# Seven products for the attention projection, its sums made behind the convolution's, and an accumulating transfer in place of the add

## Chip, cores, metric

One core of one Trainium2 chip. The metric is the device time of one execution in microseconds (us).

## What is computed

One decoder layer on 512 rows of 2048 channels, in float32. The parts that the change touches are these lines of the reference:

```python
z = jnp.einsum('bsd,dc->bsc', h, w_in[l])
cb, cc, cv, q, k, v, f_logit, gate_c, gate_a = jnp.split(z, SPLIT_POINTS, axis=-1)
conv_y = cb * causal_dwconv(cc * cv, conv_w[l])
conv_branch = jnp.einsum('bsc,cd->bsd', conv_y, w_conv_out[l])
...
attn_branch = jnp.einsum('bsc,cd->bsd', attn, w_attn_out[l])
gc = jax.nn.sigmoid(gate_c + b_gate[l, :D_MODEL])
ga = jax.nn.sigmoid(gate_a + b_gate[l, D_MODEL:])
merged = gc * conv_branch + ga * attn_branch
x = x + jnp.einsum('bsd,de->bse', merged, w_mix_out[l])
```

Both projections multiply 512 rows by a matrix of 1024 x 2048. Behind them follow the mixing projection, an MLP of width 8192 and a last norm.

## The kernel before, in words

**Precision.** A float32 operand is kept as two parts: `hi`, written by ScalarE (ACT) with a copy, and `lo`, the difference, written by VectorE (DVE). This is `split` (L100 to L102). A product of two such operands is three matmuls: hi by hi, hi by lo, lo by hi. A weight tile's parts are called `th` and `tl` in the profile; there are two buffers of each. The parts of an operand that stays (x, the convolution's result, the attention's) are made once.

**Seven products.** A `Group` (L174 to L316) multiplies a matrix of weights, cut in four quarters, by the other operand, cut likewise, with seven products of quarters instead of eight. The names of the products are those of the weights' quarters or sums: A11 and A12 (`head`), then S1, S3, S2, S4, A22 (`tail2`, L286). The sums of weights are made on the fly by DVE (`x<-x,x` or `y<-y,y`, L105). The sums of the other operand ("moving") are made beforehand. Four results come out in the order (0,0) after A12, (1,1) after S2, (0,1) after S4 and (1,0) after A22, and each goes to a function `put(i, j, v)`. `mm_cols` (L129 to L149) issues the matmuls of a product: all that use `th` first, then all that use `tl`.

**Stages around the change.** First w_in: groups m = 0 to 3 with the eight attention heads between them, m = 4 and 5 for the rest of z, m = 6 to 13 for the gates (their `put_g` applies the sigmoid on ACT, L755, and stores to `g_d`). The heads' results lie in `a_d` in HBM. Behind groups 4 to 11 the depthwise convolution is worked off, two channel tiles at a time: for q = 0 to 3, `conv_load(q)` ahead of group 4+2q loads six pieces from `z_d`; `conv_tile` (L679) computes behind group 4+2q; `conv_sums` (L691 to L704) behind group 5+2q makes the sums of the seven products, splits them, and stores eight pieces to `ys_d`. The tiles are single buffers, reused from one q to the next. So that a scheduler does not put this work too early in an engine's queue, its first instruction multiplies by a column `begin` of ones, which a tiny ACT instruction (`signal`, L662 to L667) has to read first behind a named result of a group.

**The projections** (L775 to L869). The convolution's is four branches of 512 output columns, each by seven products over a K of 1024 (`Columns`, L800): a branch takes two weight slots, y0 and y1, of three that are taken in turn. Its result times its gate is put into `held` (L832), for the fourth branch through HBM (`held_d`). The attention's is four branches by plain products (`gemm_t`, eight chunks of 128 of K); a result is multiplied by its gate (L847), added to `held`, and split into M, the operand of the mixing projection. The branches stand in the order conv 0, attn 0, conv 1, attn 1, conv 2, conv 3, attn 2, attn 3.

**What sets the order.** TensorE's order is that of the program. DVE, ACT and POOL (GpSimd) each work off one queue in order; weights are loaded by SyncE (SP), stores and the loads of sums and gates by POOL's queue.

## Time and profile before

| | |
|---|---|
| median of 3 runs | 2450.43 us (2449.39 to 2451.35) |
| the profiled execution's own time | 2452.52 us |
| its span | 2450.8 us |
| granted TensorE clock | 0.999 |
| PE, DVE, ACT, POOL busy | 99%, 80%, 48%, 9% of the span |
| the projections, conv 0 to attn 3 | 864.75 to 1031.36 us |
| group m = 7, behind which the sums of q = 1 begin | 597.40 to 635.59 us |

The profile is of one execution. PE is TensorE. A row of a timeline has the start in us, the duration in us, the engine, the line of the kernel, the operation, its output and inputs by name, and in brackets how long the engine sat idle before it and what ended that. A row of the table of windows has, for a stretch of the span, its length and each engine's busy time in it. "us to landing" of a DMA is the time from its issue until its data has arrived. PE is busy nearly all the time, so time is gained by fewer matmuls and lost by each wait that reaches PE.

### The profile page before, as it was taken

Reading aid. Unit: us, or ns where it says so; the run is one execution under the profiler, and the core shown is the slowest. Engines: PE = TensorE matmul, PEld = TensorE weight load, DVE = VectorE, ACT = ScalarE, POOL = GpSimd, SP = SyncE. Lnnn points to the kernel's source line nnn. Section 1 sums busy time; section 2 is a strip of 40 time slices with the busy share of each in tenths; the row PEclk is TensorE's granted clock in tenths of the full one; section 3 lists DMA queues with packets and bytes.
Section 4 is the critical chain, followed back from the end, with each engine's and each line's share of the span. In section 5 each row is a group of like instructions: output and inputs, shape, how many; then the busy total and the mean of one; then the engine's idle time right before and its main releaser. Section 6 shows DMA issues by size and latency. Waiting matters only on the chain.

```text
span 2450.8 us, 40086 instructions
## 1 busy us (share of the span) xinstructions
PE 2423.2 (99%) x17224; PEld 2252.6 (92%) x17224; DVE 1970.8 (80%) x1665; ACT 1180.1 (48%) x1189; POOL 230.3 (9%) x369
## 2 busy tenths in 40 slices
PE   8999999999999999999999999999999999999998
PEld 8999899999999999888899999999998888888886
DVE  7987777788887777535688898888988888889898
ACT  6443434345455544335555666666655333333334
POOL 0100000111121110000000000000011001100000
PEclk9999999999999999999999999999999999999999
DMA  7664544454656654635645646656588566655662
GB/s 250 183 192 142 154 133 146 138 160 165 211 172 214 215 186 155 216 114 205 199 169 185 231 173 216 216 202 228 177 302 293 168 247 227 237 191 183 244 225 101
DMA packets 276597, 475.62 MB, mean 194 GB/s; under 512 B 10732, under 2 KB 180836, under 8 KB 276036
## 3 DMA queue, kind: packets, MB, share of 16 engines
q1 hardware_dynamic: 232592, 291.59, 37.0%
q0 software_dynamic: 42960, 180.38, 19.8%
q8 instruction: 135, 2.21, 0.4%
q10 hardware_dynamic: 868, 1.10, 0.1%
q14 instruction: 42, 0.34, 0.0%
HBM read 374.46 MB, written 98.57 MB: 193 GB/s over the span
## 4 chain that ended last, share of the span: by engine, by line
PE 93%; DVE 3%; DMA 1%; issue 1%; ACT 1%; POOL 0%; SPq 0%; DVEq 0%; POOLq 0%; ACTq 0%
PE a L145 6%; PE a L147 6%; PE a L149 6%; PE d L149 5%; PE d L145 5%; PE d L147 5%; PE a L163 5%; PE a L165 5%; PE a L162 5%; PE c L145 4%; PE c L147 4%; PE c L149 4%; PE b L145 3%; PE b L147 3%; PE b L149 3%; PE d L165 3%
## 5 line engine op out<-in xcount | busy, mean ns | idle before, releaser
L101 ACT ACTIVATE th<-x 128x2048 fp32r<-128x2048 f32 (+1 forms) x252 | 483.4, 1918 | 462.3 <-DVE x L105 153.8
L102 DVE TENSOR_TENSOR tl<-x,th 128x2048 fp32r<-128x2048 f32 (+1 forms) x252 | 575.1, 2287 | 159.0 <-ACT th L101 144.1
L105 DVE TENSOR_TENSOR x<-x,x 128x2048 f32<-128x2048 f32 (+1 forms) x144 | 329.2, 2286 | 19.9 <-DMA x<-in_w_in_dram 16.2
L101 ACT ACTIVATE th<-y 128x2048 fp32r<-128x2048 f32 (+1 forms) x109 | 184.8, 1700 | 268.8 <-PE a L163 138.8
L102 DVE TENSOR_TENSOR tl<-y,th 128x2048 fp32r<-128x2048 f32 (+1 forms) x109 | 218.9, 2013 | 30.0 <-ACT th L101 29.5
L162 PE MATMUL a<-th,us 128*128 128x512 f32 x512 | 199.2, 389 | 0.0
L163 PE MATMUL a<-th,us 128*128 128x512 f32 x512 | 199.2, 389 | 0.0
L145 PE MATMUL a<-ST,th 128*128 128x256 f32 x752 | 174.1, 277 | 0.6 <-ACT th L101 0.6
L147 PE MATMUL a<-ST,th 128*128 128x256 f32 x752 | 173.6, 277 | 0.0
L102 DVE TENSOR_TENSOR tl<-raw,th 128x2048 fp32r<-128x2048 f32 x32 | 73.4, 2292 | 101.8 <-ACT th L101 101.5
L145 PEld LDWEIGHTS a<-ST,th 128*128 128x128 f32 x752 | 141.3, 188 | 0.9 <-ACT th L101 0.8
L147 PEld LDWEIGHTS a<-ST,th 128*128 128x128 f32 x752 | 141.3, 188 | 0.0
L165 PE MATMUL a<-tl,us 128*128 128x512 f32 x512 | 136.8, 389 | 0.0
L145 PE MATMUL c<-S,th 128*128 128x256 f32 x576 | 134.2, 278 | 0.0
L147 PE MATMUL c<-S,th 128*128 128x256 f32 x576 | 133.8, 277 | 0.0
L101 ACT ACTIVATE th<-t 128x2048 fp32r<-128x2048 f32 x31 | 59.5, 1920 | 126.1 <-DVE t L105 73.0
L145 PE MATMUL d<-ST,th 128*128 128x256 f32 x512 | 118.2, 277 | 0.0
L147 PE MATMUL d<-ST,th 128*128 128x256 f32 x512 | 118.2, 277 | 0.0
L162 PEld LDWEIGHTS a<-th,us 128*128 128x128 f32 x512 | 96.1, 188 | 20.0
L165 PEld LDWEIGHTS a<-tl,us 128*128 128x128 f32 x512 | 96.0, 188 | 20.1 <-DVE tl L102 0.2
L163 PEld LDWEIGHTS a<-th,us 128*128 128x128 f32 x512 | 96.1, 188 | 19.9
L101 ACT ACTIVATE th<-raw 128x2048 fp32r<-128x2048 f32 x32 | 61.4, 1919 | 103.0 <-PE pn L356 42.7
(362 smaller groups left out, 6517.3 us busy)
## 6 DMA issues: line engine op xcount, KB each, us to landing
x<-in_w_in_dram SPq DMA_DIRECT2D x86, 1024.0 KB, 5.9
x<-in_w_ff_dram SPq DMA_DIRECT2D x64, 1024.0 KB, 8.4
y<-in_w_ff_dram SPq DMA_DIRECT2D x64, 1024.0 KB, 8.4
us<-s_d POOLq DMA_DIRECT2D x48, 1024.0 KB, 9.2
s_d<-rh POOLq DMA_DIRECT2D x32, 896.0 KB, 5.5
s_d<-r POOLq DMA_DIRECT2D x32, 896.0 KB, 5.5
raw<-in_w_mix_out_dram SPq DMA_DIRECT2D x24, 1024.0 KB, 5.2
g_d<-o POOLq DMA_DIRECT2D x32, 256.0 KB, 3.1
```

Of the source, the lines that this page charges most:

```text
L101: nc.scalar.activation(out=hi, in_=src, func=AF.Copy, scale=one)
L102: nc.vector.tensor_tensor(out=lo, in0=src, in1=hi.bitcast(F32), op=ALU.subtract)
L105: nc.vector.tensor_tensor(out=out, in0=a, in1=b, op=ALU.subtract)
L145: nc.tensor.matmul(o, hi[:, q, js], Sh, start=first and q == 0 and j == 0, stop=False, skip_group_check=True)
L147: nc.tensor.matmul(o, hi[:, q, js], Sl, start=False, stop=False, skip_group_check=True)
L149: nc.tensor.matmul(o, lo[:, q, js], Sh, start=False, stop=q == nq - 1, skip_group_check=True)
L162: nc.tensor.matmul(o, Sh, hi[:, q, :], start=begin and q == 0, stop=False, skip_group_check=True)
L163: nc.tensor.matmul(o, Sl, hi[:, q, :], start=False, stop=False, skip_group_check=True)
L165: nc.tensor.matmul(o, Sh, lo[:, q, :], start=False, stop=q == nq - 1, skip_group_check=True)
```

## The change

Four edits.

1. **Sums of the attention.** `attention_sums(q)` stands right behind `conv_sums(q)`, in the same tiles: it loads two pieces of `a_d` by POOL, makes the same sums, splits them and stores eight pieces to `as_d`. Its first multiplication waits for a new signal at result (0,1) of group 5+2q; its other instructions have no such mark.
2. **Attention's projection by seven products.** All eight branches go through `Columns` by the function `branch`, first the four of the convolution, then the four of the attention. The plain products, the split of `a_d` and its two 2 MB tiles are gone.
3. **Adding the branches.** All 16 gated results of the convolution are stored to `held_d`. A gated result of the attention gets `held_d` added by a DMA that accumulates into the tile (POOL's queue).
4. **Parts two results later.** Such a merged quarter is split into M only behind the gate of the second result after it (a column of ones, written behind that gate, is the scale of the split's ACT copy).

Besides, the sums' pieces go into other places (4, 5, 6 for the convolution's, 0, 1, 2 and 3 for the attention's), and the first group of the MLP gets one short matmul (192 columns) ahead of its S2.

```diff
@@ -76,7 +76,8 @@
     z_d = dram.tile([3, CT, P, S], F32, name="z_d")
     g_d = dram.tile([2, KT, P, S], F32, name="g_d")
     ys_d = dram.tile([P, 2, CT // 2, 7, HS], F32, name="ys_d")
-    held_d = dram.tile([4, P, S], F32, name="held_d")
+    as_d = dram.tile([P, 2, CT // 2, 7, HS], F32, name="as_d")
+    held_d = dram.tile([KT, P, S], F32, name="held_d")
     a_d = dram.tile([CT, P, S], F32, name="a_d")
     x1_d = dram.tile([NT, P, D], F32, name="x1_d")
     s_d = [dram.tile([P, 2, 4, 7, HS], F32, name=f"s_d{i}") for i in range(DFF // 1024)]
@@ -654,15 +655,15 @@
-    begin = {(q, k): const.tile([P, 1], F32, name=f"begin{q}{k}") for q in range(CT // 2) for k in range(3)}
-    for b in begin.values():
-        nc.vector.memset(b, 1.0)
-    seen = const.tile([P, 1], F32, name="seen")
+    ones1 = const.tile([P, 33], F32, name="ones1")
+    nc.vector.memset(ones1, 1.0)
+    begin = {(q, k): ones1[:, 4 * q + k:4 * q + k + 1] for q in range(CT // 2) for k in range(4)}
+    seen = ones1[:, 32:]
     def signal(m, i, j, v):
         for q in range(CT // 2):
-            for k, place in enumerate(((4 + 2 * q, 0, 0), (4 + 2 * q, 1, 1), (5 + 2 * q, 0, 0))):
+            for k, place in enumerate(((4 + 2 * q, 0, 0), (4 + 2 * q, 1, 1), (5 + 2 * q, 0, 0), (5 + 2 * q, 0, 1))):
                 if place == (m, i, j):
                     nc.scalar.activation(out=seen, in_=v[:, 0, 0:1], func=AF.Copy, scale=begin[q, k])
@@ -688,20 +689,31 @@
             nc.vector.scalar_tensor_tensor(out=y, in0=u[:, i:S + i], scalar=w[i], in1=y, op0=ALU.mult, op1=ALU.add)
         nc.vector.tensor_tensor(out=y, in0=t["cb"], in1=y, op=ALU.mult)
-    def conv_sums(q, tiles):
-        nc.gpsimd.memset(begin[q, 2], 1.0)
-        even, odd, s13, s24 = tiles[0]["cv"], tiles[1]["cv"], tiles[0]["cc"], tiles[0]["cb"]
+    def sums_of(q, even, odd, s13, s24, his, b, dst):
+        nc.gpsimd.memset(b, 1.0)
         a11, a21, a12, a22 = even[:, :HS], even[:, HS:], odd[:, :HS], odd[:, HS:]
-        nc.vector.scalar_tensor_tensor(out=s13[:, :HS], in0=a21, scalar=begin[q, 2], in1=a22, op0=ALU.mult, op1=ALU.add)
+        nc.vector.scalar_tensor_tensor(out=s13[:, :HS], in0=a21, scalar=b, in1=a22, op0=ALU.mult, op1=ALU.add)
         sub(s13[:, HS:], a11, a21)
         sub(s24[:, :HS], s13[:, :HS], a11)
         sub(s24[:, HS:], a12, s24[:, :HS])
-        for t, h, n, w in ((even, tiles[0]["u"], 0, HS), (odd, tiles[1]["u"], 1, S), (s13, tiles[1]["cc"], 3, S),
-                           (s24, tiles[1]["cb"], 5, S)):
+        for t, h, n, w in zip((even, odd, s13, s24), his, (0, 1, 3, 5), (HS, S, S, S)):
             split(t[:, :w], h[:, :w].bitcast(F32R), t[:, :w])
             for e, o in enumerate((h, t)):
-                nc.gpsimd.dma_start(out=ys_d[:, e, q, n:n + w // HS], in_=o[:, :w].rearrange("p (n s) -> p n s", s=HS))
+                nc.gpsimd.dma_start(out=dst[:, e, q, n:n + w // HS], in_=o[:, :w].rearrange("p (n s) -> p n s", s=HS))
+    def conv_sums(q, tiles):
+        even, odd = tiles
+        sums_of(q, even["cv"], odd["cv"], even["cc"], even["cb"], (even["u"], odd["u"], odd["cc"], odd["cb"]), begin[q, 2],
+                ys_d)
+    def attention_sums(q):
+        t = {n: pq.tile([P, S], F32, tag=n, name=f"a_{n}") for n in ("cv0", "cv1", "cc0", "cb0", "u0", "u1", "cc1", "cb1")}
+        for e in range(2):
+            nc.gpsimd.dma_start(out=t[f"cv{e}"], in_=a_d[2 * q + e])
+        sums_of(q, *(t[n] for n in ("cv0", "cv1", "cc0", "cb0")), [t[n] for n in ("u0", "u1", "cc1", "cb1")], begin[q, 3],
+                as_d)
     def apart(i, name="S4", row=4):
@@ -727,6 +739,7 @@
                     conv_tile(q, e, pairs_in[q][e])
             else:
                 conv_sums(q, pairs_in.pop(q))
+                attention_sums(q)
     n = 0
     for g in (4, 2, 0, 5, 3, 1):
@@ -748,6 +761,22 @@
         behind(n)
         n += 1
+    YS, AS = {}, {}
+    def load_sums_of(t, src, ST, names, at):
+        for e in range(2):
+            nc.gpsimd.dma_start(out=t[:, e].bitcast(F32), in_=src[:, e, :, at:at + len(names)])
+        for e, n in enumerate(names):
+            ST[n] = moving(t[:, :, :, e])
+    def load_pieces(src, ST, places, touch=lambda t: None):
+        for place, (names, at) in zip(places, ((("A11", "A12"), 0), (("S1", "S3"), 3), (("S2", "S4"), 5))):
+            t = main.tile([P, 2, CT // 2, 2, HS], F32R, tag=f"t{place}", name="sums")
+            touch(t[:, 0, 0, 0, 0:1])
+            touch(t[:, 1, 0, 0, 0:1])
+            load_sums_of(t, src, ST, names, at)
     for f in range(0, KT, 2):
         def put_g(i, j, v, f=f, n=n):
             for b in range(2):
@@ -757,13 +786,11 @@
             signal(n, i, j, v)
         if n == 4 + CT:
             ph.close()
             ph = ExitStack()
-            pr = ph.enter_context(phase("pr"))
-            araw = [pr.tile([P, 4, S], F32, tag=f"araw{i}", name="araw") for i in range(2)]
-            for i, raw in enumerate(araw):
-                nc.sync.dma_start(out=raw, in_=a_d[4 * i:4 * i + 4].rearrange("k p s -> p k s"))
+            pc_ = ph.enter_context(phase("pc"))
+            y22 = pc_.tile([P, 2, CT // 2, 1, HS], F32R, tag="y22", name="ys")
+            load_sums_of(y22, ys_d, YS, ("A22",), 2)
         ahead(n)
         whole(Group(w_in, COL_GC + f * P, COL_GA + f * P, HS, Q1.moving, mm_cols, steady(n), put_g,
                     extra=apart(4, "S2", 0)))
@@ -772,28 +799,7 @@
...
+    load_pieces(ys_d, YS, (4, 5, 6))
     cycle[:], turns[0] = [i for i in free if i != 1], 2
@@ -813,60 +819,73 @@
         def done(self, *ij):
             self.at.pop(ij)
...
+    QUARTERS = ((0, 0), (1, 1), (0, 1), (1, 0))
+    def pieces(src, c, i, j):
+        k = 4 * c + 2 * j
+        return src[k:k + 2, :, i * HS:(i + 1) * HS].rearrange("k p s -> p k s")
+    def branch(view, ST, c, put):
+        whole(Columns(view, c * S, c * S + HS, HS, ST.get, mm_cols, tuple((4 * (c % 2) + b,) for b in range(4)), put,
+                      extra={"A11": "first", "S3": "first"}))
+    for c in range(4):
         gates = {}
...
+        for ij in QUARTERS:
+            gates[ij] = pc_.tile([P, 2, HS], F32, tag="hg", name="gates", bufs=4)
+            nc.gpsimd.dma_start(out=gates[ij], in_=pieces(g_d[0], c, *ij))
+        def put_conv(i, j, v, c=c, gates=gates):
+            nc.vector.tensor_tensor(out=v, in0=v, in1=gates[i, j], op=ALU.mult)
+            nc.gpsimd.dma_start(out=pieces(held_d, c, i, j), in_=v)
+            if c == 0 and not AS:
+                load_pieces(as_d, AS, (0, 1, 2), lambda t: nc.scalar.activation(out=t, in_=v[:, 0, 0:1], func=AF.Copy))
+        branch(w_conv_out, YS, c, put_conv)
+    rest3 = main.tile([P, 2, D], F32R, tag="t3", name="sums")
+    load_sums_of(rest3[:, 0].rearrange("p (e q n s) -> p e q n s", e=2, n=1, s=HS), as_d, AS, ("A22",), 2)
+    gates3 = rest3[:, 1].rearrange("p (n k s) -> p n k s", n=4, s=HS).bitcast(F32)
+    M = {}
+    M[0, 0], M[1, 0], M[0, 1] = (eights(pair(i, F32R, "m"), HS) for i in (4, 6, 5))
     ph.close()
     ph = ExitStack()
     pc_ = ph.enter_context(phase("pm"))
     M[1, 1] = eights(pc_.tile([P, 2, D], F32R, tag="h", name="m"), HS)
-    attn_out(2, lower)
-    attn_out(3, upper)
+    lags, waiting = [], []
+    for c in range(4):
+        for n, ij in enumerate(QUARTERS):
+            nc.gpsimd.dma_start(out=gates3[:, n], in_=pieces(g_d[1], c, *ij))
+        def put_attn(i, j, v, c=c):
+            g = gates3[:, QUARTERS.index((i, j))]
+            n = 16 + 4 * c + QUARTERS.index((i, j))
+            lag = ones1[:, n:n + 1]
+            if len(waiting) == 2:
+                nc.vector.scalar_tensor_tensor(out=v, in0=v, scalar=lags[0], in1=g, op0=ALU.mult, op1=ALU.mult)
+                nc.gpsimd.memset(lags[0], 1.0)
+                waiting.pop(0)(lags.pop(0))
+            else:
+                nc.vector.tensor_tensor(out=v, in0=v, in1=g, op=ALU.mult)
+            nc.gpsimd.dma_start(out=v, in_=pieces(held_d, c, i, j), accum_op=ALU.add)
+            def parts_of(one):
+                hi, lo = M[i, c // 2]
+                k = (4 * c + 2 * j) % 8
+                split(v, hi[:, k:k + 2, :], lo[:, k:k + 2, :], one)
+            lags.append(lag)
+            waiting.append(parts_of)
+        branch(w_attn_out, AS, c, put_attn)
+    for f in waiting:
+        f(1.0)
@@ -1094,6 +1113,7 @@
     g0 = ff1(0, ((5,), (0,), (1,), (7,)))
+    g0.extra.update(apart(3, "S2", 0))
     g0.head(True, rest)
     Q2.sums(3)
     g0.tail2()
```

DVE, end of group m = 7 and start of m = 8, before. `x10`, `x00` and so on are weight quarters, `tl_6831` is the lo part of A22 of group 7, `tl_6928` of A11 and `tl_6983` of A12 of group 8; `cb` is the last piece of the convolution's sums; `o` are results.

```order
L102 TENSOR_TENSOR tl_6773<-x11_6598,th_6772 128x2048
L108 TENSOR_TENSOR o_6709<-c_6601,o_6709 128x512
L102 TENSOR_TENSOR cb_6041<-cb_6041,cb_6048 128x512
L102 TENSOR_TENSOR tl_6831<-x10_6481,th_6830 128x2048
L108 TENSOR_TENSOR o_6709<-a_6483,o_6709 128x512
L102 TENSOR_TENSOR tl_6928<-x00_6922,th_6927 128x2048
L108 TENSOR_TENSOR o_6824<-a_6483,o_6824 128x512
L105 TENSOR_TENSOR x00_6922<-x01_7039,x00_6922 128x2048
L105 TENSOR_TENSOR x01_7039<-x11_7041,x01_7039 128x2048
L108 TENSOR_TENSOR o_6766<-d_6655,o_6766 128x512
L102 TENSOR_TENSOR tl_6983<-x10_6924,th_6982 128x2048
```

The same place after the change. `a_cv0`, `a_cv1` are the two loaded pieces of the attention, `a_cc0` and `a_cb0` their sums.

```order
L103 TENSOR_TENSOR cb_6051<-cb_6051,cb_6058 128x512
L106 TENSOR_TENSOR a_cc0_6920<-a_cv0_6918 128x256
L103 TENSOR_TENSOR tl_6842<-x10_6491,th_6841 128x2048
L109 TENSOR_TENSOR o_6719<-a_6493,o_6719 128x512
L103 TENSOR_TENSOR tl_6970<-x00_6964,th_6969 128x2048
L109 TENSOR_TENSOR o_6834<-a_6493,o_6834 128x512
L106 TENSOR_TENSOR x00_6964<-x01_7081,x00_6964 128x2048
L696 SCALAR_TENSOR_TENSOR a_cc0_6920<-a_cv0_6918,ones1_2789,a_cv1_6919 128x256
L106 TENSOR_TENSOR x01_7081<-x11_7083,x01_7081 128x2048
L109 TENSOR_TENSOR o_6776<-d_6665,o_6776 128x512
L106 TENSOR_TENSOR a_cb0_6921<-a_cc0_6920,a_cv0_6918 128x256
L103 TENSOR_TENSOR tl_7025<-x10_6966,th_7024 128x2048
```

One sum of the attention, which only needs the loaded piece, now stands ahead of A22's lo part; two more stand between it and A12's lo part.

POOL's queue at the same place, before: stores of the convolution's sums, then the loads of z for q = 2.

```order
L704 DMA ys_d_73<-cv_6050 128x512
L704 DMA ys_d_73<-cc_6042 128x512
L704 DMA ys_d_73<-cb_6048 128x512
L674 DMA cv_6909<-z_d_71 128x512
L674 DMA cc_6915<-z_d_71 128x512
L674 DMA cc_6908<-z_d_71 128x512
L704 DMA ys_d_73<-cb_6041 128x512
L674 DMA cb_6914<-z_d_71 128x512
L674 DMA cv_6916<-z_d_71 128x512
```

After the change, the stores of the convolution's sums and the loads of `a_d`:

```order
L703 DMA ys_d_73<-cv_6053 128x256
L703 DMA ys_d_73<-cv_6060 128x512
L703 DMA ys_d_73<-cc_6052 128x512
L703 DMA ys_d_73<-cb_6058 128x512
L714 DMA a_cv0_6918<-a_d_76 128x512
L714 DMA a_cv1_6919<-a_d_76 128x512
L703 DMA ys_d_73<-cb_6051 128x512
```

The loads of `a_d` stand where the loads of z stood, behind the stores that free their tiles. A little further on in the same queue, from the third of the attention's stores on:

```order
L694 MEMSET ones1_2789 128x1
L703 DMA as_d_74<-a_cc1_6924 128x512
L785 DMA g_d_72<-o_6776 128x2x256
L703 DMA as_d_74<-a_cv0_6918 128x256
L703 DMA as_d_74<-a_cb1_6925 128x512
L703 DMA as_d_74<-a_cv1_6919 128x512
L703 DMA as_d_74<-a_cc0_6920 128x512
L703 DMA as_d_74<-a_cb0_6921 128x512
L675 DMA cv_6951<-z_d_71 128x512
L675 DMA cb_6956<-z_d_71 128x512
L675 DMA cc_6950<-z_d_71 128x512
L675 DMA cb_6949<-z_d_71 128x512
```

The loads of z for q = 2 now stand behind all the stores of the attention's sums.

DVE in the convolution's fourth branch before, from the first sum of weights that needs its second weight tile (`y0<-y1,y0`) to the sum for S2 (`y1<-y1,y0`); `held` and `gates` are the gating.

```order
L105 TENSOR_TENSOR y0_10495<-y1_10562,y0_10495 128x1024
L108 TENSOR_TENSOR o_10421<-d_10358,o_10421 128x512
L102 TENSOR_TENSOR tl_10532<-y0_10495,th_10531 128x1024
L832 TENSOR_TENSOR held_10257<-o_10421,gates_10255 128x2x256
L105 TENSOR_TENSOR y1_10562<-y1_10562 128x1024
L102 TENSOR_TENSOR tl_10568<-y0_10495,th_10567 128x1024
L108 TENSOR_TENSOR o_10528<-b_10530,o_10528 128x512
L102 TENSOR_TENSOR tl_10598<-y1_10562,th_10597 128x1024
L832 TENSOR_TENSOR o_10528<-o_10528,gates_10487 128x512
L105 TENSOR_TENSOR y1_10562<-y1_10562,y0_10495 128x1024
```

DVE in a branch of the attention after the change, from the same sum to the row ahead of the sum for S2. `o_10602` and `o_10701` are results of two results ago, `m` the operand of the mixing projection, `ones1` the scale that orders the split.

```order
L106 TENSOR_TENSOR y0_10812<-y1_10882,y0_10812 128x1024
L103 TENSOR_TENSOR m_10557<-o_10602,m_10557 128x512
L109 TENSOR_TENSOR o_10733<-d_10670,o_10733 128x512
L103 TENSOR_TENSOR tl_10849<-y0_10812,th_10848 128x1024
L871 SCALAR_TENSOR_TENSOR o_10733<-o_10733,ones1_2789,sums_10554 128x512
L103 TENSOR_TENSOR tl_10888<-y0_10812,th_10887 128x1024
L103 TENSOR_TENSOR m_10558<-o_10701,m_10558 128x512
L106 TENSOR_TENSOR y1_10882<-y1_10882 128x1024
L109 TENSOR_TENSOR o_10845<-b_10847,o_10845 128x512
L871 SCALAR_TENSOR_TENSOR o_10845<-o_10845,ones1_2789,sums_10554 128x512
L103 TENSOR_TENSOR tl_10918<-y1_10882,th_10917 128x1024
L103 TENSOR_TENSOR m_10557<-o_10766,m_10557 128x512
```

Between the two sums of weights there stand three rows more than before, the splits `m`.

57 lines of the change are left out of this document (removed).

## Prediction

> **What bounds the kernel now.** I read the head of the page first, then the chain of waits, then the table of windows over the two stretches that the diff touches.
>
> ```profile
> span 2450.8 us, 40086 instructions
> PE 2423.2 (99%) x17224; PEld 2252.6 (92%) x17224; DVE 1970.8 (80%) x1665; ACT 1180.1 (48%) x1189; POOL 230.3 (9%) x369
> PE 93%; DVE 3%; DMA 1%; issue 1%; ACT 1%; POOL 0%; SPq 0%; DVEq 0%; POOLq 0%; ACTq 0%
> ```
>
> TensorE is busy 99% of the span and makes 93% of the chain that ends last. So matmuls removed are time gained, one for one, but a wait that reaches PE is time lost just as directly: there is no slack of PE that could take it in. DVE at 80% is an average; what matters is where its queue stands close to a deadline of PE.
>
> ```profile
> core 0: us, PE busy (x) PEld busy (x) DVE busy (x) ACT busy (x) POOL busy (x), PEclk, DMA share, GB/s
> 597.40:635.59 38.19, 38.19 (x339) 38.19 (x338) 33.05 (x26) 21.09 (x24) 8.72 (x18) 1.00 0.62 203
> 864.75:884.02 19.27, 19.27 (x173) 19.27 (x171) 15.82 (x16) 9.86 (x12) 5.55 (x8) 1.00 0.67 219
> 884.02:906.15 22.13, 22.11 (x98) 17.94 (x97) 14.29 (x20) 4.95 (x8) 1.45 (x2) 1.00 0.59 208
> 925.44:947.54 22.10, 22.09 (x98) 17.95 (x97) 14.27 (x20) 4.95 (x8) 1.45 (x2) 1.00 0.61 205
> 947.54:966.83 19.29, 19.29 (x171) 19.28 (x170) 17.44 (x22) 10.68 (x15) 1.45 (x2) 1.00 0.30 95
> 966.83:987.52 20.69, 20.07 (x173) 19.77 (x171) 17.66 (x19) 9.40 (x11) 2.91 (x4) 1.00 0.47 160
> 987.52:1031.36 43.84, 43.83 (x194) 35.96 (x193) 25.93 (x36) 12.63 (x18) 1.45 (x2) 1.00 0.62 219
> ```
>
> The first row is group m = 7, behind which the convolution's sums for q = 1 begin. The others are conv 0, attn 0, attn 1, conv 2, conv 3, and attn 2 with attn 3; the missing conv 1 is like conv 2. A branch by seven products takes 19.27 us when PE never waits. Conv 3, the only one that directly follows another such branch, takes 20.69: that row is the one to remember.
>
> **1. Matmuls removed: -11.0 us.** Attention's four plain branches take 22.13 + 22.10 + 43.84 = 88.07 us. By seven products, at 19.27, they are 77.1. That is the whole gross gain; the projections now last 864.75 to 1031.36, 166.6 us.
>
> **2. Eight seven-product branches in a row: +13.3, so +2.3 net.** Why conv 3 is slow shows in DVE's timeline of it, then PE's, then the weight loads:
>
> ```profile
> 968.42 1.23 DVE L105 TENSOR_TENSOR y<-y,y 128x1024 f32<-128x1024 f32 x1 [1.37 <-DMA y<-in_w_conv_out_dram]
> 969.56 0.68 DVE L108 TENSOR_TENSOR o<-d,o 128x512 f32<-128x512 f32 x1
> 976.50 2.48 DVE L105 TENSOR_TENSOR y<-y,y 128x1024 f32<-128x1024 f32 x2
> ```
> ```profile
> 978.95 0.39 PE L145 MATMUL a<-ys,th 128*128 128x256 f32 x1 [0.62 <-ACT th L101]
> ```
> ```profile
> DMA to landing us min/median/max: 5.4/5.8/6.3
> ```
>
> There are three weight slots and a branch takes two, so the second tile of the next branch needs the first slot of this one. That slot is free only when A22, the last product, has been split; then the load takes 5.4 to 6.3 us to land, DVE sat 1.37 us for it, and from there its queue runs to the sum for S2 (976.50) and PE waits 0.62 us for that product's hi part. In the old order a plain branch lay between two such branches, and its time covered the load; only conv 2 to conv 3 lacked that cover. In the new order seven of eight borders lack it. So I price conv 1, 2, 3 and attn 0 at conv 3's 20.7 each.
>
> In attn 1 and attn 2 three rows more stand in DVE's queue between the late sum and the sum for S2, the splits of merged quarters. One costs about what a row of 128x512 costs, next start less this start, 0.6 us; they and the queue ahead of them add 1.9 in attn 1, and 2.6 in attn 2 where four of them fall in, so 22.6 and 23.3. (By total work this fits: 17.66 us of DVE in conv 3 plus 4 x 0.6 is 20.1, already more than PE's 19.27.) Attn 3 as conv 3, 20.9 with its splits. Sum: 19.3 + 4 x 20.7 + 22.6 + 23.3 + 20.9 = 168.9 against 166.6: the gain of 11.0 is used up and 2.3 more. If each border costs nothing, the eight are 8 x 19.3 = 154.4; if every attention branch costs 23.3, they are 172.6. So this part lies between -12 and +6.
>
> The accumulating transfer is not in the trace. Rows near it:
>
> ```profile
> gates<-g_d POOLq DMA_DIRECT2D x16, 256.0 KB, 4.0
> held_d<-o POOLq DMA_DIRECT2D x4, 256.0 KB, 2.7
> held<-held_d SPq DMA_DIRECT2D x1, 1024.0 KB, 5.8
> ```
>
> It moves 256 KB, so between 2.7 and 5.8; I take 4.0, the load of that size from HBM. The split that needs it comes two results later, and the shortest such distance is two products (from S2's result to A22's), 2 x 19.27 / 7 = 5.5 us; the others are 8 to 14. With 0.54 for the issue (POOL's rows below) 4.0 fits: it costs 0. With 5.8 it is 0.8 late in one quarter of each branch, 3.4 in all, which I keep as the upper end; below 0 it cannot cost. Behind the last result nothing covers the last two splits: I add 0.6 us before the mixing projection. The 12 more stores to `held_d` lie on POOL, busy 9%: 0. The extra matmul of the MLP's first group has 192 columns, under 0.3 us: 0.
>
> **3. The sums behind groups 5, 7, 9, 11: +13.8.** DVE works its queue in order, and the change puts a row that needs a load (`a_cc0<-a_cv0`) ahead of the lo part of A22. When can that load land? POOL's timeline, and the landing of the z load whose place the load of `a_d` takes:
>
> ```profile
> 619.73 0.56 POOL L704 DMA_DIRECT2D ys_d<-cv  x1 [6.37 <-DVE cv L102]
> 626.78 0.54 POOL L674 DMA_DIRECT2D cv<-z_d  x1 [4.77 <-DMA ys_d<-cv]
> ```
> ```profile
> cv<-z_d POOLq DMA_DIRECT2D x1, 256.0 KB, 4.9
> ```
>
> The tile is being stored until 626.78, so the load cannot start before, and in this burst it takes 4.9: it lands at 631.7. Before the change DVE passed this place at 624, and nobody needed the z data for long after. Now everything behind waits:
>
> ```profile
> 618.68 0.42 DVE L105 TENSOR_TENSOR cb<-cv,cb 128x256 f32<-128x256 f32 x1
> 623.36 0.68 DVE L102 TENSOR_TENSOR cb<-cb 128x512 f32<-128x512 f32 x1
> 625.11 2.29 DVE L102 TENSOR_TENSOR tl<-x,th 128x2048 fp32r<-128x2048 f32 x1 [1.07 <-ACT th L101]
> 627.32 0.68 DVE L108 TENSOR_TENSOR o<-a,o 128x512 f32<-128x512 f32 x1
> 641.23 2.28 DVE L102 TENSOR_TENSOR tl<-x,th 128x2048 fp32r<-128x2048 f32 x1
> ```
> ```profile
> 633.71 0.91 ACT L755 ACTIVATE o<-o,cols 128x256 f32<-128x256 f32 x2 [2.48 <-DVE o L108]
> 634.53 1.91 ACT L101 ACTIVATE th<-x 128x2048 fp32r<-128x2048 f32 x1
> ```
> ```profile
> 644.66 1.98 PE L149 MATMUL b<-A,tl 128*128 128x256 f32 x16
> ```
>
> From the landing on, by these durations (start to start where rows follow directly): the sum 0.35, A22's lo part 2.2, a result 0.6; that result's two sigmoids 0.85 and A11's hi part 1.9 on ACT, which has itself to pass a hi part of the late piece; then on DVE A11's lo part 2.2, a result 0.6, a sum of weights 2.2, the marked sum 0.35, a sum of weights 2.2, a result 0.6, a sum 0.35, and A12's lo part 2.3. Together 16.7 us: 631.7 + 16.7 = 648.4. PE begins with A12's lo part at 644.66, so it waits 3.7 us. For q = 1, 2, 3 that is 11.2. For q = 0 group 5 is a group of z without sigmoids, so the hi part of A11 isn't held up by them: 16.7 - 2.75 = 14.0, and 1.0 us. Sum 12.2.
>
> The bounds are by the landing: the same kind of load later in this stage took 3.0 us,
>
> ```profile
> cb<-z_d POOLq DMA_DIRECT2D x1, 256.0 KB, 3.0
> ```
>
> which lands at 629.8 and costs 1.8 for each of three, 5.5 in all; and the median of two such loads in the whole stretch,
>
> ```profile
> cv<-z_d POOLq DMA_DIRECT2D x2, 256.0 KB, 6.5
> ```
>
> lands at 633.3 and costs 5.3 and 2.6: 18.5. I take 4.9 because it is that very place in the queue. The Trainium skill (DMA: Bandwidth & Descriptors, "Anatomy of one DMA — SWDGE (gpsimd) path") fits about 2.0 us plus bytes over 436 GB/s, so an estimate of 2.6 us here; the trace's 4.9 in the burst says otherwise, its 3.0 elsewhere comes near; by the fit this term would be about 4 us instead of 12.
>
> The loads of z for the next pair now stand behind eight more stores of sums on POOL, the last of which waits for DVE. Before, a convolution tile had its data a whole group early. I price the loss of that cover at 0.5 us for each of three, 1.5 in all, an estimate near its lower end, since a group of 38.19 us lies ahead of most of this work; the ends are 0 and 4 each, 4 being the wait of POOL's row at 626.78 once more.
>
> **Sum.** 2.3 + 0.6 + 12.2 + 1.5 = 16.6. The profiled execution took 2452.52 us with a span of 2450.8, 0.09% over the median of the runs, 2450.43; the change is the same on both, so 2450.4 + 16.6 = 2467 us.
>
> **The rivals.**
>
> A, the forecast, from 2456 (the early landing and a projection a few us better) to 2480 (the late landing).
>
> B, the branches keep pace: the weights land early enough that no border costs. For it: the two branches' windows show a DMA share of 0.30 and 95 GB/s, so transfers are not crowded, and 1.4 us sooner would do. Against: conv 3 at 20.69. Then 154.4 + 0.6 - 166.6 = -11.6, with 13.7 from the sums: 2452.5.
>
> C, faster: one mechanism, transfers land sooner than in the rows that I took. Its place is both waits: the load of `a_d` in 3.0 us after its issue and the second weight tile at most 4.9 after its own, instead of 5.8 to 6.3. Its price: -11.6 and +5.5, so 2444. It decides once `a_d` lands before 630.2 (3 x 2.2 = 6.7 lost, 4.9 won) and weights in under 5 us; should `a_d` land before 628.0, 16.7 us ahead of PE's 644.66, nothing is lost there and it is 2439.
>
> D, worse: z loads late by 4 us thrice (+10.5 over the forecast), and an accumulating transfer of 7.5 us, 2.5 late in one quarter of each branch (+10): 2487.
>
> That the change doesn't do what it says is no rival: the quoted orders show the loads, the sums and the later splits in place.
>
> **How the numbers follow.** A 0.58, B 0.12, C 0.18, D 0.12. The likeliest is A, 2467. The range of 2443 to 2486 leaves out half of C and half of D, and some of A's ends. A measurement of this kernel can tell about 0.2%, 4.9 us, from no change. A and D are slower; of B 0.03 is slower, 0.08 the same, 0.01 faster; of C 0.02 is the same, 0.16 faster. So faster 0.17, same 0.10, slower 0.73.
>
> **What would show it.** The chain's share of PE falls below 93%. In groups 8, 10 and 12 a wait of 3 to 4 us ahead of the matmuls with A12's lo part, put down to DVE, and at DVE an idle time of several us ahead of `a_cc0<-a_cv0` put down to the load of `a_d`. In the projections branches of 20.7 to 23.3 us, with PE waiting for the hi part of S1 or S2. It is wrong if the branches last 19.3 (step 2), if PE passes groups 8, 10 and 12 at 38.2 us each (step 3), or if DVE or ACT sits idle ahead of the splits `m` for an accumulating transfer (the 0 there).

## The result and the profile after

| | before | after |
|---|---|---|
| median | 2450.89 us (2449.39 to 2452.05, 4 runs) | 2504.18 us (2502.29 to 2504.56, 4 runs) |
| profiled execution | 2452.52 us, span 2450.8 | 2504.19 us, span 2502.4 |
| granted clock | 0.999 | 0.995 |
| ratio | | 1.022 (95% interval 1.0207 to 1.0232) |

The change costs 53 us, not the 17 that were forecast, and lies outside the range. The head of the page after:

```profile
span 2502.4 us, 41008 instructions
PE 2426.9 (97%) x17521; PEld 2264.0 (90%) x17521; DVE 2014.6 (81%) x1708; ACT 1206.1 (48%) x1233; POOL 298.6 (12%) x479
```

TensorE has fallen from 99% to 97% of a longer span: waits, as expected. The table of windows says where. First the seven groups m = 6 to 12 in one row, before and then after:

```profile
559.20:826.56 267.36, 267.36 (x2362) 267.36 (x2360) 222.41 (x166) 138.93 (x154) 43.04 (x80) 1.00 0.56 182
```
```profile
561.79:848.04 286.25, 271.91 (x2362) 268.77 (x2361) 239.44 (x200) 147.99 (x172) 69.40 (x132) 1.00 0.64 206
```

They take 18.9 us more with the same matmuls; DVE has 17 us more work and is still not full. Then the eight branches after, conv 0 to conv 3 and attn 0 to attn 3:

```profile
886.23:914.87 28.64, 22.75 (x173) 22.22 (x171) 16.70 (x18) 10.52 (x19) 9.60 (x13) 0.88 1.04 386
914.87:946.46 31.59, 21.77 (x173) 21.38 (x172) 18.67 (x21) 9.37 (x12) 7.25 (x10) 0.84 0.67 228
946.46:968.96 22.50, 20.28 (x173) 19.64 (x172) 18.48 (x21) 9.26 (x12) 5.80 (x8) 1.00 0.58 195
968.96:991.56 22.60, 20.25 (x173) 19.61 (x172) 18.47 (x21) 9.25 (x12) 4.37 (x6) 1.00 0.54 176
991.56:1014.17 22.61, 20.50 (x173) 19.86 (x172) 18.67 (x21) 9.34 (x12) 5.41 (x6) 1.00 0.54 155
1014.17:1037.66 23.49, 20.24 (x172) 19.64 (x172) 20.45 (x24) 12.06 (x16) 8.06 (x12) 1.00 0.67 165
1037.66:1062.52 24.86, 20.11 (x173) 19.52 (x172) 21.12 (x25) 11.92 (x16) 8.15 (x13) 1.00 0.70 174
1062.52:1086.21 23.69, 20.34 (x173) 19.59 (x171) 20.25 (x23) 12.19 (x15) 6.74 (x11) 1.00 0.70 178
```

Not one of them takes the 19.27 us that the matmuls need. Together they last 199.98 us, against 166.61 for the old eight: 33.4 more where 2.9 was forecast. So the balance of the two spans, 51.6 us, is 2.6 up to the start of group 6 (1.7 of it by 484 us, ahead of all that the change touches), 18.9 in groups 6 to 12, 33.4 in the projections, and 3.3 less behind them.

**The gate groups.** DVE's timeline at the place that the prediction worked through (group 7 now starts at 603.52):

```profile
629.50 0.68 DVE L103 TENSOR_TENSOR cb<-cb 128x512 f32<-128x512 f32 x1
637.69 0.42 DVE L106 TENSOR_TENSOR a_cc<-a_cv 128x256 f32<-128x256 f32 x1 [7.51 <-DMA a_cv<-a_d]
638.03 2.28 DVE L103 TENSOR_TENSOR tl<-x,th 128x2048 fp32r<-128x2048 f32 x1
643.70 2.29 DVE L103 TENSOR_TENSOR tl<-x,th 128x2048 fp32r<-128x2048 f32 x1 [2.78 <-ACT th L102]
652.26 2.28 DVE L103 TENSOR_TENSOR tl<-x,th 128x2048 fp32r<-128x2048 f32 x1
```
```profile
640.37 2.10 PE L150 MATMUL d<-A,tl 128*128 128x256 f32 x16 [0.31 <-DVE tl L103]
643.72 0.39 PE L146 MATMUL a<-A,th 128*128 128x256 f32 x1 [1.25 <-ACT th L102]
654.60 2.10 PE L150 MATMUL b<-A,tl 128*128 128x256 f32 x16 [1.10 <-DVE tl L103]
```

The first lines are DVE's, the others PE's. DVE sits idle 7.5 us ahead of the small sum; from there to the end of A12's lo part are 16.85 us (637.69 to 654.54), and PE waits three times for what stood behind that row: A22's lo part, A11's hi part (whose copy waited on ACT for a sigmoid, and that for DVE), A12's lo part.

**The projections.** DVE in conv 1, the issue of its second weight tile on SP, PE's wait, and the DMA issues from 870 to 930 us:

```profile
926.44 1.23 DVE L106 TENSOR_TENSOR y<-y,y 128x1024 f32<-128x1024 f32 x1 [11.35 <-DMA y<-in_w_conv_out_dram]
927.59 0.68 DVE L109 TENSOR_TENSOR o<-d,o 128x512 f32<-128x512 f32 x1
928.19 1.22 DVE L103 TENSOR_TENSOR tl<-y,th 128x1024 fp32r<-128x1024 f32 x1
```
```profile
910.86 0.92 SPq L816 DMA_DIRECT2D y<-in_w_conv_out_dram  x2
```
```profile
929.46 2.07 PE L150 MATMUL b<-sums,tl 128*128 128x256 f32 x8 [9.78 <-DVE tl L103]
```
```profile
sums<-as_d POOLq DMA_DIRECT2D x6, 1024.0 KB, 17.4
sums<-ys_d POOLq DMA_DIRECT2D x4, 1024.0 KB, 11.5
y<-in_w_conv_out_dram SPq DMA_DIRECT2D x6, 512.0 KB, 18.8
```

The tile is issued when A22 of conv 0 has been split and lands 15.6 us later, since the six 1 MB loads of the attention's sums, started behind conv 0's first result, run beside it (a DMA share of 1.04 in conv 0's window). PE waits for A12's lo part, a row that needs nothing of this tile but stands behind a sum that does. In conv 3, where the burst is over, the same load is issued at 964.87 and used at 972.46, 7.6 us later; in conv 3 of before it was 5.4.

In conv 0 PE waits for the last loads of the convolution's sums, issued by POOL at 890.03 and 892.33:

```profile
901.25 0.35 PE L146 MATMUL a<-sums,th 128*128 128x256 f32 x1 [1.97 <-DMA sums<-ys_d]
904.22 0.58 PE L148 MATMUL a<-sums,th 128*128 128x256 f32 x1 [2.62 <-DMA sums<-ys_d]
```

With a third wait of 1.30 these are 5.9 us; the other 3.5 of conv 0's 9.4 us over 19.27 are in PE's busy time (22.75), since the matmuls behind these waits ran at a lower clock (last section).

### The profile page after: what moved, and what is told of

The parts are those of the page before. It is cut to its first block, busy times and chain, and to the rows that moved or that the text cites. A ratio compares the mean times of both kernels' runs of the same rounds, so it can differ in the third digit from the quotient of the medians.

```text
span 2502.4 us, 41008 instructions
## 1 busy us (share of the span) xinstructions
PE 2426.9 (97%) x17521; PEld 2264.0 (90%) x17521; DVE 2014.6 (81%) x1708; ACT 1206.1 (48%) x1233; POOL 298.6 (12%) x479
## 3 DMA queue, kind: packets, MB, share of 16 engines
q0 software_dynamic: 54416, 208.69, 23.1%
## 4 chain that ended last, share of the span: by engine, by line
PE 59%; DVE 3%; DMA 3%; issue 2%; ACT 1%; POOL 0%; DVEq 0%; POOLq 0%; ACTq 0%
PE a L163 4%; PE a L164 4%; PE a L166 4%; PE a L146 4%; PE a L148 4%; PE a L150 4%; PE d L146 3%; PE d L150 3%; PE d L148 3%; PE pn L356 2%; PE d L166 2%; PE d L163 2%; PE pn L357 2%; PE pn L355 2%; PE d L164 2%
## 5 line engine op out<-in xcount | busy, mean ns | idle before, releaser
L102 ACT ACTIVATE th<-y 128x2048 fp32r<-128x2048 f32 (+1 forms) x137 | 214.6, 1569 | 321.2 <-PE a L164 138.9
L103 DVE TENSOR_TENSOR tl<-y,th 128x2048 fp32r<-128x2048 f32 (+1 forms) x137 | 253.2, 1851 | 33.7 <-ACT th L102 25.0
L106 DVE TENSOR_TENSOR y<-y,y 128x2048 f32<-128x2048 f32 (+1 forms) x57 | 104.7, 1837 | 27.0 <-DMA y<-in_w_conv_out_dram 17.8
L103 DVE TENSOR_TENSOR tl<-raw,th 128x2048 fp32r<-128x2048 f32 x24 | 55.0, 2293 | 72.9 <-ACT th L102 72.9
```

The costliest lines, as they stand in the source:

```text
L102: nc.scalar.activation(out=hi, in_=src, func=AF.Copy, scale=one)
L103: nc.vector.tensor_tensor(out=lo, in0=src, in1=hi.bitcast(F32), op=ALU.subtract)
L106: nc.vector.tensor_tensor(out=out, in0=a, in1=b, op=ALU.subtract)
```

## The experiments

Each branch below is counted from the first matmul of its A11 to that of the next branch. In the expectations, attn 3 of the kernels with four slots is given as 20.4 and 19.6: there the 1.9 us of the matmuls with A11's hi part are not counted.

**1. The sums alone.** The kernel before, with the change's `attention_sums` and the signal for it, and nothing else:

```diff
...
             else:
                 conv_sums(q, pairs_in.pop(q))
+                attention_sums(q)
```

> The kernel before with the attention's sums added behind the convolution's and stored to HBM, where nothing reads them; the projections stay as they were. Theory 1 (the whole loss in the gate groups is DVE's and ACT's wait for the load of a_d, ahead of A22's lo part): the seven groups from m = 6 to 12 take 286 us as in the changed kernel, against 267 before, and the time is 2450.9 + 20 = 2471, between 2467 and 2475. Rival (the gate groups lose because the changed projection's early loads of sums and gates crowd the DMA queues): these groups stay within 3 us of 267 and the time within 2450 to 2455.

Measured: 2471.12 us against 2450.39 (1.0081, 1.0064 to 1.0098), and for groups 6 to 12:

```profile
559.52:845.24 285.72, 275.05 (x2362) 272.26 (x2360) 239.29 (x200) 148.06 (x172) 65.20 (x126) 0.99 0.64 207
```

The whole loss of the gate groups is there without the new projections. The rival falls.

**2. The late sum.** The instructions that need only the loaded pieces get the column of ones too:

```diff
-        sub(s13[:, HS:], a11, a21)
+        if dst is as_d:
+            nc.vector.scalar_tensor_tensor(out=s13[:, HS:], in0=a11, scalar=b, in1=a21, op0=ALU.mult, op1=ALU.subtract)
+        else:
+            sub(s13[:, HS:], a11, a21)
...
-            split(t[:, :w], h[:, :w].bitcast(F32R), t[:, :w])
+            split(t[:, :w], h[:, :w].bitcast(F32R), t[:, :w], b if dst is as_d and n < 2 else 1.0)
```

> The changed kernel, but each of the attention's instructions that needs only the loaded pieces (the second sum and the two first hi parts) is also scaled by the column of ones that is written behind result (0,1). So neither DVE nor ACT meets a row that waits for a_d ahead of A22's lo part; the number of instructions is the same. Theory 1 (the wait in the queue costs): the seven groups fall from 286 to between 267 and 274, the total from 2504.2 to between 2485 and 2492. Rival (DVE has too much work there: 33 us in a group of 38.2 before, plus some 7): the wait only moves, groups at 283 or more, total 2500 or more.

Measured: 2487.47 us (1.0148, 1.0132 to 1.0163), 16.7 less than the change, and for groups 6 to 12:

```profile
560.81:830.14 269.33, 267.77 (x2362) 267.55 (x2360) 236.41 (x198) 147.76 (x173) 69.87 (x132) 1.00 0.66 216
```

With as much work on DVE, 236 us, 17 of the 18.9 us are gone. It was the place of three instructions in two queues, not their work.

**3. The burst two branches later.**

```diff
-            if c == 0 and not AS:
+            if c == 2 and not AS:
```

> The changed kernel, but the six 1 MB loads of the attention's sums are issued behind the first result of the convolution's third branch instead of its first. Theory 2 (these loads crowd out the last loads of the convolution's sums and the weights of conv 1): conv 0 and conv 1 fall from 28.7 and 31.5 us to 20 to 25 each, and conv 2 and conv 3 rise by less than half of that, because the weights of those branches are then loaded beside six loads with no others; total 2490, between 2482 and 2497. Rival (the burst costs the same wherever it lies): conv 2 and conv 3 rise by as much, total 2501 to 2508.

Measured: 2505.09 us (1.0222, 1.0207 to 1.0237). Conv 1 and conv 3:

```profile
909.75:929.82 20.07, 19.82 (x172) 19.44 (x171) 18.48 (x21) 9.26 (x12) 5.81 (x8) 1.00 0.60 190
952.29:988.65 36.36, 21.67 (x172) 21.27 (x171) 18.50 (x21) 9.32 (x12) 5.82 (x8) 0.81 0.72 249
```

Conv 1 falls from 31.59 to 20.07, as theory 2 has it, but conv 3 rises from 22.60 to 36.36: the cost moves with the burst, undiminished. Conv 0 falls only from 28.6 to 27.9, so its late sums have, in the main, another cause than the burst. In the total the rival holds.

**4. Four weight slots.** `cycle` holds three slots, and the tile x1 becomes a fourth:

```diff
+    places = iter((cycle + [1]) * 4)
...
-                self.at[i, j] = main.tile([P, 2, self.nq, self.w], F32, tag=f"x{slot()}", name=f"y{j}")
+                self.at[i, j] = main.tile([P, 2, self.nq, self.w], F32, tag=f"x{next(places)}", name=f"y{j}")
```

> The changed kernel with four weight slots in turn for the eight branches instead of three (the fourth is the tile that the changed kernel leaves idle until x is loaded), so no weight tile waits for the branch ahead of it. Theory 3 (at each border the second weight tile waits for A22's split of the branch before, then 7.5 us of landing, then DVE's queue): conv 2, conv 3 and attn 0 fall from 22.5 to 19.3 to 20.0, attn 1 to 3 from 23.5 to 24.9 down to 20 to 22, conv 1 from 31.5 to 19.5 to 25; total 2504.2 - 20 to - 30 = 2474 to 2484. Rival (DVE's own work bounds a branch, 17.7 us and more of it in 19.3): branches stay above 21.5 and the total above 2495.

Measured: 2479.11 us (1.0116, 1.0101 to 1.0131). Conv 1, conv 2 and attn 1:

```profile
907.50:935.11 27.61, 22.37 (x172) 22.18 (x171) 18.93 (x21) 9.55 (x12) 7.28 (x10) 0.88 1.05 374
935.11:954.38 19.27, 19.27 (x172) 19.27 (x171) 17.91 (x21) 9.28 (x12) 5.81 (x8) 1.00 0.54 174
992.91:1016.02 23.11, 20.20 (x172) 19.61 (x171) 20.40 (x24) 12.00 (x16) 8.06 (x12) 1.00 0.74 188
```

Conv 2, conv 3 and attn 0 take 19.27: PE never waits there. Theory 3 holds for them, and they give 9.9 of the 25 us. Conv 0 gives 5.0 (28.64 to 23.69), conv 1 4.0, and attn 1 to 3 together 4.4. The gain in conv 0 is not theory 3's: the tile x1 was free before, and two loads of x into it (1 MB, issued at 885.28 and 888.95 on POOL's queue, ahead of the last loads of the convolution's sums) stood in conv 0; with x1 in use they come at 1055.17. One of the two waits above and the low clock are gone there. No run parts these two effects of the edit. Attn 1 to 3 stay at 23.1, 22.2 and 22.3, so what is left of their loss is not the weight tile. Conv 1 is still at 27.6: with the burst as it was, DVE waits 5 us there for a gate load of 256 KB:

```profile
925.38 0.69 DVE L843 TENSOR_TENSOR o<-o,gates 128x512 f32<-128x512 f32 x1 [5.00 <-DMA gates<-g_d]
```

**5. The burst spread.** Two of the six loads behind the first result of each of conv 1, 2 and 3, three slots:

```diff
...
-            if c == 0 and not AS:
-                load_pieces(as_d, AS, (0, 1, 2), lambda t: nc.scalar.activation(out=t, in_=v[:, 0, 0:1], func=AF.Copy))
+            if c and (i, j) == (0, 0):
+                load_pieces(as_d, AS, (0, 1, 2), lambda t: nc.scalar.activation(out=t, in_=v[:, 0, 0:1], func=AF.Copy), (c - 1,))
```

> The changed kernel, but the six 1 MB loads of the attention's sums are issued two at a time, behind the first results of the convolution's second, third and fourth branch, instead of all six behind that of the first. Theory 2 (a burst of 6 MB costs because a weight tile that a border waits for is queued behind all of it): conv 1 falls from 31.6 to about 20 as it did with the later burst, and 2 MB at each of three borders cost 1 to 3 us each, no more than 30 us for any branch; total 2495 to 2500. Rival (the bytes cost the same wherever they lie): the three branches rise by 11 together, total 2502 to 2507.

Measured: 2504.65 us (1.0221, 1.0207 to 1.0235); conv 1 to attn 0 take 20.3, 28.0, 27.1 and 23.9. The rival holds again: conv 2, conv 3 and attn 0 are 11.2 us longer together than after the change, conv 1 is 11.3 shorter. As long as each border waits for a load, the megabytes put beside that load are paid, in one piece or in three.

**6. Late sum, four slots and spread loads together.**

> The changed kernel with the late sum, the four slots and the spread loads together. If the three losses stand side by side: 2504.2 - 16.7 (late sum) - 25.1 (four slots) - 8 (conv 1 from 27.6 to 19.3 to 20, since with four slots the loads no longer sit ahead of the tile that is waited for) = 2454, between 2449 and 2460: the matmuls saved are then still eaten by the late sums for conv 0 (4 us) and by attn 1 to 3, at 23.1, 22.2 and 20.4 instead of 19.3. Rival (the losses hide one another, and DVE's work is behind them all): 2465 or more.

Measured: 2454.91 us (11 runs; 1.0017, 1.0009 to 1.0026). Conv 0 and conv 1:

```profile
866.57:890.33 23.76, 20.44 (x173) 20.07 (x172) 16.90 (x18) 9.79 (x13) 5.13 (x7) 1.00 1.01 351
890.33:909.60 19.27, 19.27 (x172) 19.27 (x171) 18.22 (x21) 9.51 (x14) 7.30 (x10) 1.00 0.77 257
```

The sum comes out within 1 us: the losses stand side by side. Beside the very loads that made conv 2 and 3 take 28 and 27 us in run 5, conv 1, 2 and 3 now take 19.27 each.

**7. Splits three results later.**

```diff
-            if len(waiting) == 2:
+            if len(waiting) == 3:
```

> The combined kernel, but a merged quarter is split three results later instead of two. Theory 4 (an accumulating transfer that lands after 5 to 8 us holds up ACT's hi part of a quarter and through its queue the hi part for S3): attn 1 to 3 fall to 20 to 21 and the time by 3 to 6 us. Rival (the splits' own work on DVE and ACT is what costs): no more than 1 us either way.

Measured: 2453.21 us (11 runs; 1.0012, 1.0003 to 1.002). Attn 1 to 3 fall from 23.2, 22.4 and 22.3 to 20.3, 21.9 and 21.5, by 4.3 together, but the total only by 1.7: conv 0 was 1.5 longer in this execution, and the mixing projection now waits 2.25 us once for a lo part of its weights. The branches go as theory 4 has it; the total lies between theory 4 and the rival.

**8. No addition.** The accumulating transfer and the later place of the splits left out:

```diff
-            if len(waiting) == 2:
+            if False:
...
-            nc.gpsimd.dma_start(out=v, in_=pieces(held_d, c, i, j), accum_op=ALU.add)
...
-            waiting.append(parts_of)
+            parts_of(1.0)
```

> The combined kernel without the addition of the branches: the attention's gated result is split at once, with no accumulating transfer and nothing moved to later results, so that the convolution's branch is missing in the output. The splits' number is the same. Theory 4: attn 1 to 3 at 19.3 to 20.5, the time 4 to 7 us below the combined kernel's. Rival (the splits' own work): the attention's branches stay at 22 or more and the time within 1 us.

Measured: 2454.38 us (11 runs; 1.0009, 1.0000 to 1.0018), though the profiled execution took 2449.51. Attn 1 and 2 there:

```profile
967.17:988.53 21.36, 19.84 (x172) 19.45 (x171) 20.80 (x25) 11.59 (x16) 2.89 (x4) 1.00 0.42 121
988.53:1010.25 21.72, 20.21 (x173) 19.82 (x172) 20.74 (x25) 11.67 (x16) 2.89 (x4) 1.00 0.52 171
```

With no transfer to wait for, these branches still take 21.4 and 21.7, and DVE is busy 20.8 and 20.7 us of that. So of the 10 us that attn 1 to 3 have over 3 x 19.27 in kernel 6 some 3.4 belong, in the traces, to the transfer together with the marks and the later place of the splits, which this edit takes out as one. Of the rest, DVE's busy time accounts for what it has over 19.27, 1.5 us in each of attn 1 and 2; that it is the cause is argued here. In the total neither can be told from the spread of the runs (2449 to 2457).

**9. The lo part of M on POOL.** Kernel 7 with

```diff
-                split(v, hi[:, k:k + 2, :], lo[:, k:k + 2, :], one)
+                nc.scalar.activation(out=hi[:, k:k + 2, :], in_=v, func=AF.Copy, scale=one)
+                nc.gpsimd.tensor_tensor(out=lo[:, k:k + 2, :], in0=v, in1=hi[:, k:k + 2, :].bitcast(F32), op=ALU.subtract)
```

> The combined kernel with splits three results later, and the lo part of a merged quarter computed on POOL instead of DVE. Theory 5 (what is left in attn 1 to 3 is DVE's own work: it is busy 20.6 and 21.0 us of 23.2 and 22.4 there, more than the 19.3 that PE needs): without the four splits of 0.6 to 0.7 us each DVE has 18.2, and attn 1 to 3 fall from 20.3, 21.9 and 19.6 to 19.3 to 19.9; time 2.5 to 4 us below 2453.2. Rival (ACT's chain, or POOL's queue, in which the accumulating transfers now stand behind these subtractions): attn 1 to 3 stay or rise, time 2453 or more.

Measured: 2464.99 us (1.0062, 1.0049 to 1.0074), 12 slower than kernel 7. DVE's groups by form in attn 1 to 3 of this kernel (970 to 1043 us), and then of kernel 11 (970 to 1035), which has the lo parts on DVE (columns: busy us, mean ns):

```profile
L103 DVE TENSOR_TENSOR tl<-y,th 128x1024 fp32r<-128x1024 f32 x20 | 31.8, 1611 | 1.5 <-ACT th L102 1.5
L106 DVE TENSOR_TENSOR y<-y,y 128x1024 f32<-128x1024 f32 x8 | 19.1, 2387 | 0.2
```
```profile
L103 DVE TENSOR_TENSOR tl<-y,th 128x1024 fp32r<-128x1024 f32 x19 | 22.9, 1220 | 1.5 <-ACT th L102 1.4
L106 DVE TENSOR_TENSOR y<-y,y 128x1024 f32<-128x1024 f32 x8 | 9.8, 1221 | 0.1
```

DVE's same instructions take up to twice as long. Where POOL subtracts twice, the timelines of the two engines show it directly:

```profile
996.83 3.45 POOL L887 TENSOR_TENSOR m<-o,m 128x512 fp32r<-128x512 f32 x2
```
```profile
995.01 6.35 DVE L103 TENSOR_TENSOR tl<-y,th 128x1024 fp32r<-128x1024 f32 x2
```

Two DVE rows, 2.36 us together in the change's conv branches, become 6.35: 4 us more beside 3.45 us of POOL's work. This way of taking work from DVE gives more back to it than it takes, so theory 5 was not tested as it was meant. But the run says something on it: against kernel 7, attn 1 to 3 take 11.8 us more (75.4 against 63.6), and DVE is busy 11.2 us more in them (71.9 against 60.7). DVE time that is added there is paid nearly one for one; that less of it would shorten the branches, no run shows.

**10 and 11. The rest of the sums later.** The last piece of the attention's sums and its first gates (2 MB) are loaded behind conv 1's last result; 10 with the lo parts on POOL, 11 with them on DVE:

```diff
...
             nc.gpsimd.dma_start(out=pieces(held_d, c, i, j), in_=v)
+            if c == 1 and (i, j) == (1, 0):
+                rest_late(v)
```

> The kernel with the lo parts on POOL, and the last piece of the attention's sums and its first four gates (2 MB) loaded behind conv 1's last result instead of during the last gate group. Theory 2 for conv 0 (its sums for S2 and S4 arrive late because 2 MB that nobody needs yet share the queues): conv 0 falls from 25.3 and 23.8 us to 20.5 to 22.5, the time by 1.5 to 4 against the kernel without this edit, so 2446 to 2449: below the kernel before. Rival (that load comes late because its place is free late, whatever shares the queues): conv 0 stays within 1 us of 23.8.

Measured: 2459.37 us (1.0037, 1.0024 to 1.0051), 5.6 under kernel 9, with conv 0 at 20.5 instead of 23.9: theory 2 holds for conv 0, while the total, which started from the slow DVE, is above what was expected.

> The combined kernel with splits three results later, lo parts on DVE again, and the last piece of the attention's sums and its first gates loaded behind conv 1. If the edits add up: conv 0 at 20.6 instead of 25.3 (as with the lo parts on POOL), attn 1 to 3 at 20.3, 21.9 and 19.6, so 2453.2 - 4 = 2449, between 2447 and 2452: the same as the kernel before. If the loss in conv 0 only moves into later branches: 2453 or more.

Measured: 2449.44 us against 2450.59 (11 and 15 runs; 0.9994, 0.9985 to 1.0003). Conv 0 and attn 1 to 3:

```profile
867.92:888.79 20.87, 19.92 (x173) 19.72 (x172) 16.94 (x18) 9.81 (x13) 5.13 (x7) 1.00 0.88 296
966.13:986.60 20.47, 20.03 (x173) 19.64 (x172) 19.62 (x23) 10.89 (x14) 7.99 (x11) 1.00 0.83 210
986.60:1008.26 21.66, 19.83 (x172) 19.43 (x171) 20.94 (x25) 12.10 (x16) 8.09 (x12) 1.00 0.75 188
1008.26:1029.76 21.50, 19.83 (x173) 19.44 (x171) 20.16 (x23) 12.90 (x16) 8.19 (x13) 1.00 0.68 168
```

This is the best version with the seven products: 55 us under the change and level with the kernel before. Its projections take 161.8 us (867.92 to 1029.76), 4.8 less than before's 166.6, but they start 3.2 us later than before's.

**12. The short matmul alone.** The kernel before with the change's line `g0.extra.update(apart(3, "S2", 0))`.

> The kernel before with one line of the change: the matmul of 192 columns ahead of S2 in the MLP's first group. In the profile of before the matmuls of 256 columns that follow S2's late start there come every 0.118 us until the group's end, and after the change every 0.113, and the rest of the kernel behind the mixing projection is 3.3 us shorter. Theory 6 (the short matmul sets the pace): 2.0 to 3.0 us below before, 2447.5 to 2448.5, and 135 matmuls in 15 us instead of 130 in that stretch. Rival (the pace comes with something else that the change did, such as the time since the last wait): within 1 us of before.

Measured: 2450.61 us against 2449.67 (1.0001, 0.9992 to 1.001). The pace did come, 135 matmuls in 15 us as after the change:

```profile
1275.00:1290.00 15.00, 15.00 (x135) 15.00 (x134) 10.28 (x9) 9.32 (x8) 1.07 (x2) 1.00 0.92 314
```

but the total shows no gain. In that one execution 2.7 us were won in the group and 1.7 had been lost between 597 and 1219 us. Theory 6 is right on the pace and unproven on the time, and so the 3.3 us behind the projections stay unexplained.

## Why the prediction was wrong

- **Direction.** Slower was forecast with a chance of 0.73, for the right two reasons. The size was missed, 53 instead of 17.
- **Step 1, the matmuls.** Right: in run 6 conv 1, 2, 3 and attn 0 take 19.27 each. It needs four slots to be seen.
- **Step 2, the step that failed.** "So I price conv 1, 2, 3 and attn 0 at conv 3's 20.7 each" carried the landing of 5.4 to 6.3 us from the old order, where only one border had such a load, into one with 6 MB more of loads. The loop named there (A22's split, the load, DVE's queue) is what run 4 shows, but a branch lasts as long as the landing and some 15 us of DVE's chain, an estimate from the traces: 5.4 gives 20.4, 7.6 gives 22.6, and 15.6 gives over 30. The diff's loads of `ys_d` and its six loads of `as_d` behind conv 0's first result were there to be read, and no term of the sum was for them: conv 1 took 31.6, 10.9 us over its price, and runs 3 and 5 show that this cost goes where the burst goes. What makes 7.6 of 5.4 at the later borders, 1.8 to 1.9 us in each of conv 2, conv 3 and attn 0, no run takes apart. A DMA share of 0.30 (rival B's evidence) was that of conv 2 before; conv 3's own row has 0.47, and conv 0 after has 1.04.
- **Conv 0** was taken as 19.3 and took 28.6. That its last sums land late had no term in the sum. Two causes are shown: 2 MB for much later share the queues (conv 0 falls by 4.4 us from run 7 to run 11, by 3.4 from 9 to 10), and with four slots, which also move x's loads away, it falls by 5.0 (run 4). That the places of these sums come free late is argued, and no run tests it. Conv 0 and conv 1 make 20 of the 31 us by which the branches exceed their prices.
- **Attn 1 and 2** were forecast at 22.6 and 23.3 and took 23.5 and 24.9; attn 3, at 20.9, took 23.7. The splits' rows in DVE's queue are there, and without transfer and marks the branches still take 21.4 and 21.7 (run 8). The accumulating transfer was mis-sized: it landed after 4.1 to 8.6 us, median 6.2, where 4.0 was taken and 5.8 was the upper end, and its issue took 1.2 us, not 0.54. Yet the 0 for it holds in this kernel's branches: ACT waits for it only behind the last branch, 4.2 us in two waits, and PE does not wait there. Ahead of the other splits ACT waits, where it waits, for the mark or a gate's load. With the other losses gone (kernel 6) ACT waits once in attn 1 to 3 for the transfer, 1.4 us, and 2.3 us once with no releaser shown, and the later splits of run 7 give 4.3 us back in the trace.
- **Step 3.** The mechanism held in each part: the load landed 5.1 us after its issue (4.7 to 5.5; 4.9 was taken), and the chain from there to A12's lo part was 16.85 us (16.7). For q = 1 the end of that part came 3.8 us after PE's need. What was short is the rest: A11's hi part and a result for S4 were late as well, so q = 1 to 3 cost 4.6, 4.9 and 5.9 us instead of 3.7, and q = 0 cost 3.5 instead of 1.0: its chain took 15.5 us where 14.0 were counted, and a result for S4 came 1.3 us late. Together 18.9 against 12.2 and 1.5. The 1.5 us for late loads of z no run shows by itself: with the late sum (run 2) these loads stand behind the same stores, and the seven groups lose 2.0 us in all. The Trainium skill (DMA: Bandwidth & Descriptors, "Anatomy of one DMA — SWDGE (gpsimd) path") gives an estimate of 2.6 us for this load; the runs show 5.1, and the estimate doesn't hold beside other traffic.
- **The rivals.** B and C rested on transfers that land sooner; they landed later. D named late transfers, but not the ones that cost.
- **The bounds.** With every attention branch at 23.3 the sum is 19.3 + 3 x 20.7 + 4 x 23.3 = 174.6, not 172.6, so the upper end of step 2 was +8; and the wait of POOL's row at 626.78 is 4.8, not 4. Neither moves the forecast or reaches the measured time.

## What to carry to other kernels

When a load's wait closes a loop (slot free, load, work, slot free), price the loop with the landing that the new traffic will give, not with that of a quiet row; or give it one more slot: here that edit was worth 25 us, x's loads moved by it included, and in run 6 conv 1, 2 and 3 then took 19.27 each beside 2 MB of other loads. An instruction that needs only a load can be put far ahead in an in-order queue, and there it holds everything behind it: mark it so that it stands where its data is surely there (16.7 us for three small marks). Seven products save TensorE's time only if the engine that makes the sums has room: in run 8 DVE is busy 20.8 us in an attention branch for which TensorE needs 19.3.
